# A two-layer decoder trunk on one core: the value and gate products of the gMLP layer split otherwise, and their order and engines changed

## The chip, the core and the metric

The program runs on one core of a Trainium2 chip. The metric is the device time of one execution in microseconds (us); lower is better. A core has TensorE (PE, matrix products, with its weight loads shown as PEld), VectorE (DVE), ScalarE (ACT) and GpSimd (POOL), each of which works through its own list of instructions in order and waits on semaphores for the others. SyncE (SP) issues the DMA transfers that bring inputs from memory (HBM) into the on-chip SBUF. TensorE writes to PSUM, eight banks of 128 x 512 floats, from which VectorE and ScalarE read.

## The reference

The trunk has 512 tokens of width 1024 and two layers, each a token mixer followed by a squared-ReLU MLP, with RMS norms and residual sums. The first mixer is the one that the change touches:

```python
def gmlp_mixer(h, w_in, ln_g, ln_b, w_s, b_s, w_out):
    z = jax.nn.gelu(h @ w_in)               # 512 x 4096
    u, v = jnp.split(z, 2, axis=-1)         # gates u, values v: 512 x 2048 each
    v = layer_norm(v, ln_g, ln_b)
    v = v.reshape(B, S // CHUNK, CHUNK, GMLP_GROUPS, GMLP_GROUP_DIM)
    w = jnp.where(causal[None], w_s, jnp.zeros((), w_s.dtype))
    s = jnp.einsum('gts,bnsgc->bntgc', w, v) + b_s.T[None, None, :, :, None]
    out = u * s.reshape(B, S, GMLP_WIDTH)
    return out @ w_out
```

The second mixer is forgetting attention; both MLPs have 4096 hidden columns. Everything is float32.

## The kernel before, in words

**Products in three parts.** Each float32 operand is split into a rounded high part and the remainder. ScalarE makes the high part (`wh`, `xh`, `gth`, `vh`), VectorE or GpSimd subtracts it to get the low part (`wl`, `xl`, `gtl`, `vl`), and `mm3` (L297) adds three matmuls, high by high, high by low and low by high. So a weight chunk of 128 x 1024 that arrives by DMA (`raw`) costs ScalarE one instruction (L104) and VectorE one (L105) before TensorE can use it. `Stream` holds the list of all chunks; `take` hands out the next one and splits those up to three ahead, with three `raw` buffers and four pairs of `wh` and `wl`.

**2x2 products.** Where two column blocks and two halves of the contraction are at hand, seven half-size products with sums and differences of the operands (Strassen-Winograd) take the place of eight. The sums of the weights are formed on the chip, and so are those of the tokens (`token_sums`, L456; results `gth`, `gtl`).

**The gMLP layer before** has two sections. In the values section TensorE first makes four plain gate blocks (`pu`, 96 matmuls of 512 columns, two chunks interleaved so that work starts with the first block of `x`), and then, twice, a 2x2 product over two groups of 512 value columns (loop over `n` at L521; tiles `v0a` to `v1d`; 7 x 24 = 168 matmuls of 512 columns each time). Of each group of four weight blocks for such a product the four sums are made by `sum_parts` (L449) on GpSimd. `keep` and `join` (L523, L527) move the results to `v`, apply GELU and take statistics. In the gates section come two plain gate blocks (`("u", 2)` in `GMLP_ORDER`, 48 matmuls of 512 columns) and five 2x2 gate pairs (`gate_pair`, L579; tiles `da`, `bc`; 7 x 12 = 84 matmuls of 256 columns each; their weight sums, L133 to L136, on GpSimd). Between these, `mix(cb)` (L642) treats one block of 128 value columns: four ScalarE instructions normalise it (L655, by `lnr` and `lnm`), one makes its high part (L658), GpSimd the low part (L659), TensorE multiplies by the causal weights (`sp`, eight matmuls, L671 and L672), VectorE adds the terms (L661, L674, L675), GpSimd multiplies by the gate `u` (L677), and the result is split into `zg` and `zl` (L684, L685). `out_chunk` (`po`) multiplies four such blocks by the output weights, 24 matmuls of 512 columns for each of 16 chunks, and adds to `x`. The squared sums of the norm go through GpSimd and four small matmuls (`nps`), the spread root through four more (`npb`).

**What sets the order.** `GMLP_ORDER` is the order in which the Python code issues pairs ("uu"), single mixes ("s"), mixing weights ("w") and output chunks ("o"); the numbers in a "uu" entry are the mixes after its four quarters. The scheduler that builds the program then places each engine's instructions, and moves them ahead where it reckons them ready; `tc.issue_after(x)` keeps it from placing an instruction ahead of `x`. Engines run their lists strictly in this order on the chip. The later parts, the MLPs and the attention layer, have an order of their own.

Of the kernel before, what the change touches and what calls it, by code (L numbers as in the profile page):

```python
# [8 lines left out]
F32 = mybir.dt.float32  # L9
# [53 lines left out]
class Stream:  # L63
# [22 lines left out]
    def _load(self):  # L86
# [8 lines left out]
        if i not in self.halved:  # L95
            self.issued[i] = self.nc.sync.dma_start(t[:, :n], src)

    def piece(self, i, e):
        t, n = self.raw[i]
        sl = self._pieces(i, n)[e]  # L100
        self.nc.sync.dma_start(t[:, sl], self.chunks[i][0][:, sl])
# [5 lines left out]
    def _split(self):  # L107
# [17 lines left out]
        if isinstance(src, tuple) and src in self.after:  # L125
            self.after.pop(src)()
# [48 lines left out]
def trunk(ctx: ExitStack, tc: tile.TileContext, A, out, stages=4):  # L175
# [226 lines left out]
    nm = Norm(0)  # L402
    for b in range(KB):
        nm.block(b, squared=False)
        if b == 0:
            ws.prefetch(2)
        if b == 3:
            fourth = nm.high.ins

    with ExitStack() as st:  # L410
# [13 lines left out]
        def u_place(b, dt, name):  # L424

            n, e = divmod(b, 2)
            if n == 0:
                return small.tile([P, S], dt, tag="sqs", name=f"{name}{b}", bufs=2)
            if n in (1, 5):
                return gp.tile([P, S], dt, tag=f"u1_{e}", name=f"{name}{b}")  # L430
            return gq.tile([P, S], dt, tag=f"u{(n - 2) % 4}_{e}", name=f"{name}{b}")
# [6 lines left out]
        with ExitStack() as st2:  # L438
# [4 lines left out]
            def load_part(n, q, c):  # L443
                g, at = {1: (1, 2), 2: (0, 0), 4: (0, 2), 3: (1, 0)}[q]
                t = vp.tile([P, CHUNK_COLS], F32, tag=f"s{q}_{c}", name=f"gs{n}_{q}_{c}")
                nc.sync.dma_start(t, A["gw_v"][2 * n + g, at + c])
                parts[n, q, c] = ws.made[n, q, c] = t

            def sum_parts(n, c):  # L449
                s1, s2, s4, s3 = (parts[n, q, c] for q in (1, 2, 4, 3))  # L450
                pool.tensor_tensor(s1, s3, s1, op=ALU.add)
# [20 lines left out]


            pu = [psA(f"pu{b}") for b in range(4)]
            two = [[t.rearrange("p (k m) -> p k m", m=P) for t in ws.take()] for _ in range(2)]
            for k in range(KB):
                for b, (wh, wl) in enumerate(two):
                    mm3(pu[b], wh[:, k], wl[:, k], nm.h[k], nm.l[k], k == 0, k == KB - 1)
            with tc.issue_after(fourth):
                for b in range(KB):  # L480
                    nm.square(b)
            with tc.issue_after(ws.issued[3].ins):
                for c in range(2):
                    for q in (3, 1, 2, 4):
                        load_part(0, q, c)
            dense_a(pu[2], ws.take(), nm)
            nm.finish()
            with tc.issue_after(nm.squared.ins):
                for k in range(4):
                    token_sums(k)  # L490
            with tc.issue_after(nm.root.ins):
                for c in range(2):
                    sum_parts(0, c)
            dense_a(pu[3], ws.take(), nm)
            nm.spread()
            for b in range(4):
                us[b] = u_place(b, F32, "u")
                gated(pu[b], us[b])
# [16 lines left out]
            def columns(i, g):  # L515
                return v[g][:, :, i]

            def blocks(t):
                return t.rearrange("p (b n) -> p b n", n=P)

            for n in range(2):  # L521

                def keep(i, j, src):  # L523
                    for e in range(2):
                        act.activation(columns(2 * j + e, 2 * n + i), blocks(src[e]), AF.Copy)

                def join(i, j, src):  # L527
                    for e in range(2):
                        t, g = 2 * j + e, 2 * n + i
                        vs = columns(t, g)  # L530
                        dve.tensor_tensor(vs, blocks(src[e]), vs, op=ALU.add)
                        act.activation(vs, vs, AF.Gelu_apprx_tanh, scale=nm.rstd[:, t : t + 1])
                        dve.bn_stats(bn[:, t, g], vs)

                pairs = {}

                def bank(w, *kinds):
                    pairs[w] = [kind(f"v{n}{w}{e}") for e, kind in enumerate(kinds)]

                if n == 0:  # L540
                    bank("a", psB, psB), bank("b", psB, psD), bank("d", psA, psA), bank("c", psA, psA)
                else:
                    bank("c", psB, psB), bank("b", psB, psD), bank("d", psA, psA), bank("a", psA, psA)
                a, b, c_, d = (pairs[w] for w in "abcd")
                if n == 0:
                    for q in (1, 2, 4, 3):
# [690 lines left out]
```

## Time and profile before

| | before |
|---|---|
| median of 3 runs | 1299.96 us (1299.83 to 1300.64) |
| the profiled execution | 1299.96 us, span 1298.2 us |
| TensorE busy | 1258.0 us, 97% of the span |
| VectorE busy | 921.9 us, 71% |
| ScalarE busy | 688.3 us, 53% |
| GpSimd busy | 552.8 us, 43% |
| mean granted clock of TensorE | 0.993 |

The profile is of one execution. Times in its views count from the start of the span. A view by stretches gives each engine's busy time in it; a timeline lists instructions with start and duration, and in brackets the idle time before one and what ended it; a view of waits adds up that idle time by what ended it; a view of groups gives count, total and mean duration by line and operation. Matmuls overlap in the pipeline, so what one costs is the distance between starts, not its duration.

### The profile page before, as it was taken

The page shows a single profiled execution, that of the slowest core. Times are in us where ns is not written, and L with a number is a line of the kernel's source. Part 1 is how long each engine was busy: PE and PEld are TensorE (multiplying, and loading weights), DVE is VectorE, ACT ScalarE, POOL GpSimd, SP SyncE. Part 2 cuts the span into 40 slices and gives each one's busy share as a digit, 9 for nine tenths or more (in the row PEclk, how much of TensorE's full clock was granted, in tenths as well). Part 3 has the DMA queues.
Part 4 walks back from the last instruction along what each step waited for, and adds up shares of the span by engine and source line. Part 5 has one row for each costly group of instructions (what it writes and reads, how often), then busy time and mean ns, then how long its engine had stood idle before and what let it go on. Part 6 is the DMA issues. An engine that isn't in the chain of part 4 may idle for free.

```text
span 1298.2 us, 18918 instructions
## 1 busy us (share of the span) xinstructions
PE 1258.0 (97%) x7247; PEld 1112.1 (86%) x7247; DVE 921.9 (71%) x1190; ACT 688.3 (53%) x1121; POOL 552.8 (43%) x422
## 2 busy tenths in 40 slices
PE   8699789999999999999999999999999999999998
PEld 7477778878889998999899999899788989999987
DVE  7988687898777676675635666766897867676763
ACT  6565864437444444343457777778474434444430
POOL 4762535635532323230357666667364422222200
PEclk9899999999999999999999999999999999999999
DMA  8352133232333232323223223223313332332321
GB/s 325 109 176 69 37 101 109 61 121 81 101 111 113 82 116 80 131 79 117 67 82 124 90 86 102 82 81 99 98 56 123 100 112 98 98 112 84 114 82 65
DMA packets 43595, 132.21 MB, mean 102 GB/s; under 512 B 5416, under 2 KB 7520, under 8 KB 43504
## 3 DMA queue, kind: packets, MB, share of 16 engines
q1 hardware_dynamic: 43216, 130.98, 31.2%
q8 instruction: 57, 0.93, 0.3%
q14 instruction: 34, 0.28, 0.1%
q10 hardware_dynamic: 288, 0.02, 0.0%
HBM read 128.82 MB, written 2.16 MB: 101 GB/s over the span
## 4 chain that ended last, share of the span: by engine, by line
PE 83%; DVE 8%; ACT 4%; issue 2%; POOL 2%; DMA 1%; SPq 0%; DVEq 0%; POOLq 0%; ACTq 0%
PE po L290 36%; PE da L290 12%; PE bc L290 9%; PE pq L290 9%; PE pg L290 3%; PE ph L290 3%; DVE wl L105 2%; PE ot L290 2%; PE lg L290 2%; ACT v L655 1%; PE v1a L290 1%; PE tp L295 1%; PE pv L290 1%; PE v0a L290 1%; PE v1c L290 1%
## 5 line engine op out<-in xcount | busy, mean ns | idle before, releaser
L104 ACT ACTIVATE wh<-raw 128x1024 fp32r<-128x1024 f32 (+3 forms) x236 | 223.8, 950 | 207.8 <-PE po L290 96.3
L105 DVE TENSOR_TENSOR wl<-raw,wh 128x1024 fp32r<-128x1024 f32 (+1 forms) x184 | 274.4, 1506 | 19.9 <-ACT wh L104 19.5
L290 PE MATMUL po<-zl,wh 128*128 128x512 f32 x640 | 251.5, 393 | 2.0 <-DVE zl L747 1.2
L290 PE MATMUL po<-zh,wl 128*128 128x512 f32 x512 | 201.9, 394 | 0.0
L290 PE MATMUL po<-zh,wh 128*128 128x512 f32 x512 | 199.7, 391 | 0.0
L803 DVE TENSOR_TENSOR x<-x,po 128x512 f32<-128x512 f32 x128 | 87.2, 682 | 105.5 <-PE po L290 105.4
L105 POOL TENSOR_TENSOR wl<-raw,wh 128x768 fp32r<-128x768 f32 (+3 forms) x52 | 103.2, 1985 | 125.1 <-ACT wh L104 122.6
L146 POOL TENSOR_TENSOR ssum<-raw 128x512 f32<-128x512 f32 x26 | 36.4, 1400 | 270.0 <-DMA raw<-in_m_dram 260.4
L290 PEld LDWEIGHTS po<-zl,wh 128*128 128x128 f32 x640 | 120.5, 188 | 25.1 <-DVE zl L747 1.5
L104 ACT ACTIVATE sh<-ssum 128x1024 fp32r<-128x1024 f32 x52 | 55.2, 1061 | 163.2 <-POOL ssum L147 94.4
L290 PEld LDWEIGHTS po<-zh,wl 128*128 128x128 f32 x512 | 96.3, 188 | 19.1
L290 PEld LDWEIGHTS po<-zh,wh 128*128 128x128 f32 x512 | 96.4, 188 | 18.2
L290 PE MATMUL pq<-wh,xh 128*128 128x384 f32 (+2 forms) x256 | 88.2, 344 | 0.0
L290 PE MATMUL pq<-wh,xl 128*128 128x384 f32 (+2 forms) x256 | 83.1, 325 | 0.0
L290 PE MATMUL pq<-wl,xh 128*128 128x384 f32 (+2 forms) x256 | 82.9, 324 | 0.0
L105 DVE TENSOR_TENSOR sl<-ssum,sh 128x1024 fp32r<-128x1024 f32 x52 | 65.9, 1268 | 17.7 <-ACT sh L104 17.6
L148 POOL TENSOR_TENSOR ssum<-raw,ssum 128x512 f32<-128x512 f32 x26 | 37.2, 1430 | 66.7 <-DVE sl L105 66.3
L290 PE MATMUL da<-th,sl 128*128 128x256 f32 x208 | 58.9, 283 | 0.0
L290 PE MATMUL da<-tl,sh 128*128 128x256 f32 x208 | 58.7, 282 | 0.0
L290 PE MATMUL da<-th,sh 128*128 128x256 f32 x208 | 58.7, 282 | 0.0
L783 DVE TENSOR_TENSOR zc<-da,sl 128x512 f32<-128x512 f32 x26 | 18.0, 692 | 55.2 <-PE da L290 55.2
L149 POOL TENSOR_TENSOR ssum<-raw,raw 128x512 f32<-128x512 f32 x26 | 56.2, 2162 | 0.0
(336 smaller groups left out, 3658.5 us busy)
## 6 DMA issues: line engine op xcount, KB each, us to landing
raw<-in_m_dram SPq DMA_DIRECT2D x128, 512.0 KB, 3.7
gs<-in_gw_v_dram SPq DMA_DIRECT2D x16, 512.0 KB, 5.7
raw<-in_gw_o_dram SPq DMA_DIRECT2D x16, 512.0 KB, 3.6
raw<-in_fw_qkv_dram SPq DMA_DIRECT2D x20, 384.0 KB, 3.2
raw<-in_gw_u_dram SPq DMA_DIRECT2D x14, 512.0 KB, 3.6
raw<-in_gw_v_dram SPq DMA_DIRECT2D x12, 512.0 KB, 3.6
raw<-in_fw_g_dram SPq DMA_DIRECT2D x8, 512.0 KB, 3.5
cb<-cd SPq DMA_DIRECT2D x16, 256.0 KB, 3.3
```

The costliest lines, as they stand in the source:

```text
L104: self.nc.scalar.activation(hi, t, AF.Copy)
L105: eng.tensor_tensor(lo, t, hi.bitcast(F32), op=ALU.subtract)
L146: tt(s12[:, 0], a21, a22, op=ALU.add)
L148: tt(s43[:, 0], a12, s12[:, 1], op=ALU.subtract)
L149: tt(s43[:, 1], a11, a21, op=ALU.subtract)
L290: ins = pe.matmul(dst, a, b, start=start, stop=stop, skip_group_check=more)
L295: placed(pe.transpose(dst, src, ident[: src.shape[0], : src.shape[0]]), 256)
L655: act.activation(vb[:, i], vb[:, i], AF.Identity, scale=lnr[:, i : i + 1], bias=lnm[:, i : i + 1])
L783: dve.tensor_tensor(z[:, 1].rearrange("p (j t) -> p j t", j=2), a.unsqueeze(1).to_broadcast([P, 2, HS]), late.rearrange("p (j t) -> p j t" ...
L803: dve.tensor_tensor(x[b], x[b], pt, op=ALU.add)
```

## The change

The values section starts with plain products for the first two groups of 512 columns (192 matmuls of 512 columns, tiles `pv`), and only the other two groups are a 2x2 product (168). Their weight sums, now eight instructions in place of sixteen, are on VectorE. The four plain gate blocks at the start and the two in the gates section are gone: all 16 gate blocks are eight 2x2 pairs (8 x 84 matmuls of 256 columns), all after the values. The two first chunks of the stream are still loaded in halves. The normalising instructions of block `cb` may stand no earlier than behind the high part of block `cb - 1`. Line numbers move by 5 to some 35 (the splits L104 and L105 become L99 and L100, `mm` L290 becomes L275).

```diff
-GMLP_ORDER = [("w", 0), ("u", 2), ("uu", 3, None, 0, 1, 2), ("uu", 4, 3, None, None, None)]
-GMLP_ORDER += [("o", 0, 0), ("s", 4), ("o", 0, 1), ("s", 5), ("o", 0, 2), ("o", 0, 3)]
...
+GMLP_ORDER = [("w", 0), ("uu", 0, None, None, None, None), ("uu", 1, None, None, 0, None), ("uu", 2, None, 1, 2, None)]
+GMLP_ORDER += [("uu", 3, 3, None, None, None), ("o", 0, 0), ("s", 4), ("o", 0, 1), ("s", 5), ("o", 0, 2), ("o", 0, 3)]
+GMLP_ORDER += [("uu", 4, 6, 7, None, None), ("w", 1), ("o", 1, 0), ("o", 1, 1)]
...
-    ws.load(2)
     load_x(0)
-    ws.piece(0, 0)
-    ws.piece(1, 0)
...
+    ws.load(1)
+    for b in range(1, KB):
         load_x(b)
...
+            def load_parts(c):
+                for q, (g, at) in ((3, (3, 0)), (1, (3, 2)), (2, (2, 0)), (4, (2, 2))):
+                    parts[q, c] = ws.made[q, c] = vp.tile([P, CHUNK_COLS], F32, tag=f"s{q}_{c}", name=f"gs{q}_{c}")
+                    nc.sync.dma_start(parts[q, c], A["gw_v"][g, at + c])
+
+            def sum_parts(c):
+                s1, s2, s4, s3 = (parts[q, c] for q in (1, 2, 4, 3))
+                dve.tensor_tensor(s1, s3, s1, op=ALU.add)
+                dve.tensor_tensor(s3, s2, s3, op=ALU.subtract)
+                dve.tensor_tensor(s2, s1, s2, op=ALU.subtract)
+                dve.tensor_tensor(s4, s4, s2, op=ALU.subtract)
...
+            def normal(i, g, src):
+                vs = columns(i, g)
+                act.activation(vs, src, AF.Gelu_apprx_tanh, scale=nm.rstd[:, i : i + 1])
+                dve.bn_stats(bn[:, i, g], vs)
+
+            for g in range(2):
+                pv = [(psB if g == 1 and i < 3 else psA)(f"pv{g}_{i}") for i in range(NT)]
+                for c in range(4):
+                    wh, wl = (t.rearrange("p (k n) -> p k n", k=2) for t in ws.take())
+                    for i in range(NT):
+                        for kk in range(2):
+                            k = 2 * c + kk
+                            mm3(pv[i], nm.h[k][:, tok[i]], nm.l[k][:, tok[i]], wh[:, kk], wl[:, kk], k == 0, k == KB - 1)
...
+                    if g == 0 and c > 1:
+                        with tc.issue_after(ws.issued[2 * c + 2].ins):
+                            load_parts(c - 2)
+                    if g == 1 and c in (1, 2):
+                        sum_parts(c - 1)
...
+            with tc.issue_after(now["vh"]) if cb else ExitStack():
+                for i in range(NT):
+                    act.activation(vb[:, i], vb[:, i], AF.Identity, scale=lnr[:, i : i + 1], bias=lnm[:, i : i + 1])
...
+            now["vh"] = act.activation(vh, vb, AF.Copy).ins
...
+            with tc.issue_after(lnm_made.ins):
+                dve.scalar_tensor_tensor(b2, now["rs"][:, g * P : (g + 1) * P], lngb[:, 1, cb : cb + 1], now["b"], op0=ALU.mult, op1=ALU.add)
```

**Three places in the built order.** First GpSimd before, in the values section, behind the root of the norm (`rstd`); `gs` are the weight blocks of a 2x2 product:

```order
L344 TENSOR_TENSOR rstd_344<-ms_342,mhalf 128x4
L451 TENSOR_TENSOR gs_1_0_293<-gs_3_0_291,gs_1_0_293 128x1024
L451 TENSOR_TENSOR gs_1_1_301<-gs_3_1_299,gs_1_1_301 128x1024
L452 TENSOR_TENSOR gs_3_0_291<-gs_2_0_295,gs_3_0_291 128x1024
L452 TENSOR_TENSOR gs_3_1_299<-gs_2_1_303,gs_3_1_299 128x1024
L453 TENSOR_TENSOR gs_2_0_295<-gs_1_0_293,gs_2_0_295 128x1024
```

Now VectorE has them, between the splits (`wl`) and the token sums (`t`, `gt`, `gtl`) of the same section:

```order
L444 TENSOR_TENSOR t_377<-gx_375 128x256
L446 SCALAR_TENSOR_TENSOR t_377<-x_91,gains,t_377 128x256
L445 SCALAR_TENSOR_TENSOR gt_376<-x_91,gains,gx_375 128x256
L431 TENSOR_TENSOR gs_0_332<-gs_0_330,gs_0_332 128x1024
L100 TENSOR_TENSOR wl_341<-raw_166,wh_340 128x1024
L447 SCALAR_TENSOR_TENSOR gt_376<-x_91,gains,t_377 128x256
L451 TENSOR_TENSOR gtl_201<-t_377,gth_197 128x512
L432 TENSOR_TENSOR gs_0_330<-gs_0_334,gs_0_330 128x1024
```

The sums have left GpSimd's list and stand one by one among VectorE's other work. Second, ScalarE before, at the first mix; `v` are the value blocks, `vh` the high part of one, `u` a gate:

```order
L436 ACTIVATE u_1079<-u_1079 128x512
L655 ACTIVATE v_175<-v_175,lnm,lnr 128x128 x16
L655 ACTIVATE v_176<-v_176,lnm,lnr 128x128
L658 ACTIVATE vh_1198<-v_175 128x512
L104 ACTIVATE wh_1116<-raw_937 128x1024
L655 ACTIVATE v_176<-v_176,lnm,lnr 128x128
L436 ACTIVATE u_1113<-u_1113 128x512
```

and now:

```order
L417 ACTIVATE u_980<-u_980 128x512
L623 ACTIVATE v_193<-v_193,lnm,lnr 128x128 x4
L99 ACTIVATE wh_951<-raw_825 128x1024
L626 ACTIVATE vh_1118<-v_193 128x512
L623 ACTIVATE v_193<-v_193,lnm,lnr 128x128 x2
L417 ACTIVATE u_981<-u_981 128x512
L623 ACTIVATE v_193<-v_193,lnm,lnr 128x128 x2
L555 ACTIVATE gse_1010<-da_1008 128x256
```

Four normalisations stand ahead of the first high part, in place of seventeen. Third, VectorE now, at the first mix (`sp` to `zt`) in the second gate pair, with the splits of the weights that follow:

```order
L643 SCALAR_TENSOR_TENSOR zt_1124<-sp_0_1125,lngb,b_1122 128x256
L643 SCALAR_TENSOR_TENSOR zt_1124<-sp_1_1132,lngb,b_1122 128x256
L644 SCALAR_TENSOR_TENSOR zt_1124<-sp_0_1125,lngb,zt_1124 128x256
L644 SCALAR_TENSOR_TENSOR zt_1124<-sp_1_1132,lngb,zt_1124 128x256
L630 SCALAR_TENSOR_TENSOR b_1307<-rs_1109,lngb,bs_1297 128x128
L100 TENSOR_TENSOR wl_1001<-raw_803,wh_1000 128x1024
L100 TENSOR_TENSOR wl_1005<-raw_926,wh_1004 128x1024
```

and TensorE there (`da` is half of the pair's result):

```order
L641 MATMUL sp_1_1132<-wsb_873,vl_1119 128x128
L640 MATMUL sp_1_1132<-wsb_873,vh_1118 128x256
L641 MATMUL sp_1_1132<-wsb_873,vl_1119 128x128
L275 MATMUL da_1008<-gth_197,wh_1000 128x256
L275 MATMUL da_1008<-gtl_201,wh_1000 128x256
L275 MATMUL da_1008<-gth_197,wl_1001 128x256
```

The split `wl_1001`, which the third product behind the mix needs, stands on VectorE behind the five instructions of the mix.

More of the change, by code (lines that the diff above doesn't have):

```diff
@@ L94, in _load @@
         self.raw[i] = (t, n)
[L95 to L101, printed above, removed]
+        for sl in self._pieces(i, n):
+            self.issued[i] = self.nc.sync.dma_start(t[:, sl], src[:, sl])
     def _parts(self, hi, lo, t, eng):
@@ L424, in u_place @@
         def u_place(b, dt, name):
[L426 to L431, printed above, removed]
+            return gq.tile([P, S], dt, tag=f"u{b % 8}", name=f"{name}{b}")
         def gated(pu, u):
@@ L471, in token_sums @@
                     dve.tensor_tensor(l, t, h.bitcast(F32), op=ALU.subtract)
[L474 to L498, printed above, removed]
+            def columns(i, g):
+                return v[g][:, :, i]
+            def blocks(t):
+                return t.rearrange("p (b n) -> p b n", n=P)
+            def normal(i, g, src):
+                vs = columns(i, g)
+                act.activation(vs, src, AF.Gelu_apprx_tanh, scale=nm.rstd[:, i : i + 1])
+                dve.bn_stats(bn[:, i, g], vs)
@@ new lines, in trunk @@
+            for g in range(2):
+                pv = [(psB if g == 1 and i < 3 else psA)(f"pv{g}_{i}") for i in range(NT)]
[5 more added lines that the diff above has]
+                            mm3(pv[i], nm.h[k][:, tok[i]], nm.l[k][:, tok[i]], wh[:, kk], wl[:, kk], k == 0, k == KB - 1)
+                    if g == 0 and c == 2:
+                        with tc.issue_after(fourth):
+                            for b in range(KB):
+                                nm.square(b)
+                        nm.finish()
+                    if g == 0 and c == 3:
+                        nm.spread()
+                        with tc.issue_after(nm.squared.ins):
+                            for k in range(4):
+                                token_sums(k)
+                    if g == 0 and c > 1:
[4 more added lines that the diff above has]
+                for i in range(NT):
+                    normal(i, g, blocks(pv[i]))
@@ L513, in sums @@
                 return lambda k: [t[k][:, q - 1] for t in (th, tl)]
[L515 to L546, printed above, removed]
-                        for c in range(2):
-                            ws.after[0, q, c] = lambda q=q, c=c: load_part(1, q, c)
-                product(a, half(0, 0))
-                keep(0, 0, a)
-                product(b, half(1, 0))
-                join(0, 0, b)
-                product(d, sums(4))
-                keep(1, 0, d)
-                product(c_, sums(1))
-                keep(1, 1, c_)
-                product(a, sums(2), True)
-                keep(0, 1, a)
-                product(c_, half(1, 1), True)
-                if n == 0:
-                    for c in range(2):
-                        sum_parts(1, c)
-                join(0, 1, c_)
-                product(a, sums(3), True)
-                join(1, 0, a)
-                join(1, 1, a)
@@ new lines, in trunk, with keep, join @@
+            a, b = ([psA(f"v{w}{e}") for e in range(2)] for w in "ab")
+            c_, d = [psB(f"vc{e}") for e in range(2)], [psB("vd0"), psD("vd1")]
+            def keep(i, j, src):
+                for e in range(2):
+                    act.activation(columns(2 * j + e, 2 + i), blocks(src[e]), AF.Copy)
+            def join(i, j, src):
+                for e in range(2):
+                    vs = columns(2 * j + e, 2 + i)
+                    dve.tensor_tensor(vs, blocks(src[e]), vs, op=ALU.add)
+                    normal(2 * j + e, 2 + i, vs)
@@ L568, in trunk @@
+            product(a, half(0, 0))
+            keep(0, 0, a)
+            product(b, half(1, 0))
+            join(0, 0, b)
+            product(d, sums(4))
+            keep(1, 0, d)
+            product(c_, sums(1))
+            keep(1, 1, c_)
+            product(a, sums(2), True)
+            keep(0, 1, a)
+            product(c_, half(1, 1), True)
+            join(0, 1, c_)
+            product(a, sums(3), True)
+            join(1, 0, a)
+            join(1, 1, a)
         gq = st.enter_context(tc.tile_pool(name="gq", bufs=1))
@@ L689, in trunk @@
         for kind, n, *at in GMLP_ORDER:
[L690 to L696 removed]
+            if kind == "w":
                 mixing_weights(n)
```

64 lines of the change are left out of this document (17 added, 47 removed).

## The prediction

> **What bounds the kernel now.** I read the span, then busy time by stretches, then TensorE's waits, then the timelines around the two longest, and last the prices.
>
> ```profile
> span 1298.2 us, 18918 instructions
> ```
> The profiled execution took 1299.96 us, exactly the median of the three runs; 1.8 us lie outside its span. From the first MLP on, all engines have the same instructions in the same order before and after, so only the gMLP layer, the first 311.9 us, can change of itself. The stretches follow; the columns are length, then busy time of TensorE, its weight loads, VectorE, ScalarE and GpSimd, then the granted clock.
>
> ```profile
> 0.00:311.90 311.90, 280.94 (x1450) 236.79 (x1451) 253.43 (x308) 176.46 (x284) 158.11 (x94) 0.97 0.37 121
> 30.95:125.75 94.80, 81.61 (x346) 64.62 (x344) 84.84 (x72) 53.99 (x70) 55.67 (x20) 0.95 0.39 123
> 125.75:311.90 186.15, 171.71 (x987) 150.01 (x986) 146.16 (x207) 102.31 (x182) 89.85 (x61) 0.98 0.28 85
> 137.00:171.00 34.00, 22.97 (x149) 20.66 (x148) 21.45 (x30) 34.00 (x80) 13.47 (x11) 0.91 0.20 61
> 250.00:275.00 25.00, 21.59 (x135) 18.72 (x134) 24.76 (x34) 13.31 (x22) 12.79 (x9) 1.00 0.42 127
> ```
> TensorE is the bound, yet idle for 31 us of the layer (311.9 less 280.94): 13.2 us in the values (second row), 14.4 us in the gates (third), 11.0 of these between 137 and 171, where ScalarE is busy all the time. TensorE's waits, longest first (total, times, longest):
>
> ```profile
> PE v0a L290 <- DVE wl L105: 10.6, 1, 10.6
> PE po L290 <- ACT wh L104: 4.0, 1, 4.0
> PE sp L671 <- DVE zt L675: 3.0, 3, 1.5
> PE sp L671 <- DVE u L607: 2.3, 1, 2.3
> ```
> The 10.6 us end with VectorE's split at 42.33. VectorE's and GpSimd's timelines (start, duration) show why:
>
> ```profile
> 23.50 0.86 DVE L464 TENSOR_TENSOR t<-gx 128x256 f32<-128x256 f32 x1 [1.94 <-ACT gx L460]
> ...
> 31.78 2.88 DVE L471 TENSOR_TENSOR gtl<-gt,gth 128x512 fp32r<-128x512 f32 x1
> ...
> 42.33 3.36 DVE L105 TENSOR_TENSOR wl<-raw,wh 128x1024 fp32r<-128x1024 f32 x1
> ...
> 124.29 1.22 DVE L105 TENSOR_TENSOR wl<-raw,wh 128x1024 fp32r<-128x1024 f32 x1 [0.43 <-ACT wh L104]
> ```
> ```profile
> 31.62 5.26 POOL L451 TENSOR_TENSOR gs<-gs,gs 128x1024 f32<-128x1024 f32 x2
> ```
> A split takes 1.22 us with GpSimd quiet and 3.36 us beside GpSimd's weight sums of 2.63 us each. The second idle stretch begins after this:
>
> ```profile
> 125.43 2.48 DVE L531 TENSOR_TENSOR v<-v1a,v 128x512 f32<-128x512 f32 x4
> ```
> ```profile
> 136.00 6.66 ACT L655 ACTIVATE v<-v,lnm,lnr 128x128 f32<-128x128 f32 x17 [3.13 <-DVE lnm L577]
> ```
> From the last value join to the first normalisation are 10.6 us; then ScalarE makes 17 normalisations (0.39 us each) before it forms the first block's high part.
>
> **The change part by part.** Prices of TensorE are starts over count in the chain of waits: 24 value products, 24 plain gate products, 24 half-width ones, 24 of the output. Then the first and last row of four of a mix's eight products.
>
> ```profile
> 109.24 5.60 PE v1a L290 x24
> ...
> 125.91 5.48 PE pu L290 x24
> ...
> 235.31 2.85 PE da L290 x24
> ...
> 306.59 5.49 PE po L290 x24
> ```
> ```profile
> 144.75 0.33 PE L671 MATMUL sp<-wsb,vh 128*128 128x256 f32 x1
> ...
> 145.26 0.22 PE L672 MATMUL sp<-wsb,vl 128*128 128x128 f32 x1
> ```
> That is 0.233, 0.228, 0.119 and 0.229 us, and 2 x 0.51 = 1.0 us a mix. The marks of the layer are its first product, the sum of squares (0.8 us, and the spread of the root as much), the first gate product and the first of the MLP:
>
> ```profile
> 5.17 0.51 PE L290 MATMUL pu<-xh,wh 128*128 128x512 f32 x1 [0.39 <-ACT wh L104]
> ...
> 27.73 0.95 PE L290 MATMUL nps<-ones,sqs 128*128 128x2 f32 x8
> ...
> 125.75 0.39 PE L290 MATMUL pu<-xh,wh 128*128 128x512 f32 x1
> ...
> 311.93 0.40 PE L290 MATMUL ph<-xh,wl 128*128 128x512 f32 x1
> ```
>
> Products. Three plain gate pairs leave (144 x 0.228 = 32.9 us) and three split ones come (252 x 0.119 = 29.9); a plain value pair has 24 products more (5.6 us). TensorE gains 2.6 us of work.
>
> Values before: 5.2 + 96 x 0.228 + 336 x 0.233 + 1.6 = 107.1; they ended at 125.75, so 18.7 us were waiting and low clock. After: the first product still needs only the first x block and the first half chunk, in the same place of the queue; a step of k then takes 12 products (2.8 us) for 512 KB, where six products (1.4 us) took 384 KB. I allow 0.5 us of waits and get 5.2 + 360 x 0.233 + 1.6 + 0.5 = 91.3.
>
> VectorE's sums are eight instructions; the nearest row is the undisturbed split of the same size, 8 x 1.22 = 9.8 us; the upper bound is 8 x 3.36 = 26.9, the lower nothing, while GpSimd is quiet. Three of them stand before the split of the eighth chunk, which TensorE needs after 170 products, at about 46.5. VectorE reaches its first token sum at about 23.5 as now (the first row), and has some 11 us of sums, splits and token sums up to the end of that split: 12 us of cover. At the upper bound of the three sums (10.1 for 3.7) 5 us are left; behind it the splits for the 2x2 pair take VectorE 1.22 us per 2.8 us of TensorE. So nothing on the path, and up to 10 us if that cover is gone.
>
> Gates before: 125.75 + 48 x 0.228 + 420 x 0.119 + 384 x 0.229 + 0.9 + 16 x 1.0 = 291.6, with 0.9 for the four row-sum products; they ended at 311.9, so 20.3 us waited. After, the work is 672 x 0.119 + 87.8 + 0.9 + 16.3 = 184.8, which would end at 276.1. What waits are left decides. VectorE's rows in the gate stretch (total, mean ns of one):
>
> ```profile
> L105 DVE TENSOR_TENSOR wl<-raw,wh 128x1024 fp32r<-128x1024 f32 x33 | 48.9, 1488 | 5.1 <-ACT wh L104 5.0
> L388 DVE TENSOR_TENSOR x<-x,po 128x512 f32<-128x512 f32 x31 | 20.4, 678 | 12.6 <-PE po L290 12.6
> L675 DVE SCALAR_TENSOR_TENSOR zt<-sp,lngb,zt 128x256 f32<-128x256 f32 x32 | 14.0, 473 | 0.0
> L674 DVE SCALAR_TENSOR_TENSOR zt<-sp,lngb,b 128x256 f32<-128x256 f32 x32 | 13.9, 476 | 0.7
> L685 DVE TENSOR_TENSOR zl<-zt,zg 128x512 fp32r<-128x512 f32 x16 | 12.9, 803 | 8.0 <-ACT zg L684 7.9
> L435 DVE TENSOR_TENSOR u<-u,rbc 128x512 f32<-128x512 f32 x10 | 12.1, 1213 | 0.1
> ...
> L661 DVE SCALAR_TENSOR_TENSOR b<-rs,lngb,bs 128x128 f32<-128x128 f32 x16 | 5.4, 340 | 5.5 <-PE rs L648 5.5
> L105 DVE TENSOR_TENSOR wl<-raw,wh 128x512 fp32r<-128x512 f32 x5 | 5.0, 1002 | 0.3 <-ACT wh L104 0.3
> ...
> L435 DVE TENSOR_TENSOR u<-pu,rbc 128x512 f32<-128x512 f32 x2 | 1.4, 692 | 1.0 <-PE pu L290 0.9
> ```
> A split pair costs VectorE 3 x 1.488 + 1.002 + 2 x 0.678 + 2 x 1.213 = 9.2 us, a mix 0.34 + 2 x 0.476 + 2 x 0.473 + 0.803 = 3.0, an output chunk 1.488 + 2 x 0.678 = 2.8. The first four pairs with four mixes have 49 us of VectorE against 45 of TensorE (336 x 0.119 + 4.1 + 0.9): at least 4 us of waiting. Step by step it is more. The chain from the last join to the first high part is 10.6 + 4 x 0.39 + 0.6 = 12.8 us; two full and one half split of the gates now stand in it (4.0), so it ends 16.8 us after the values, while TensorE comes to the first mix after 129 half-width products and the row sums, 15.8; the third weights of the second pair then wait on ScalarE behind those normalisations: 2.5 us in all. Next, TensorE needs the split of the second pair's last weights, and VectorE has four instructions of the mix (1.9), one of 0.34 and that split (1.49) in a row: 3.3 us. The third pair repeats a third of this (1.1), the first and fourth lose 0.5 and 1.0. Sum 8.4 us. The upper bound is the present hand-over, 11.0 us idle over two pairs, so 22 for four.
>
> The last four pairs, twelve mixes and the output have 140 us of TensorE beside 118 of VectorE, with output chunks between the pairs; two pairs back to back lost 3.4 us (250 to 275). I take 2, from 0 to 7. Low clock and gaps too small for the list: 2.5, since 34 us at 0.91 cost about 3. The layer then ends at 276.1 + 8.4 + 2 + 2.5 = 289.0, earlier than 311.9 by 22.9; 1299.96 - 22.9 gives **1277 us**.
>
> Normalising a block ahead costs nothing: the same 64 instructions in another order; its new wait holds ScalarE's other work only behind a high part that is due first.
>
> The low clock has a page: the Trainium skill, TensorE: Matmul & The Clock Gate, HAM oscillation, has the clock drop only after idle gaps over about 3.4 us. By it none of the waits that I expect would cost clock, and the sum would be 1274.5. In the stretch at 0.91 the longest wait was 4.0 us, so this trace does not contradict it.
>
> **The rivals.** *A, nearly no waits in the gates* (0 to 6 us): for it, the stretch after 235 packed two pairs with little loss; against it, VectorE's 49 against 45. 1264 to 1270.
> *B, the hand-over keeps its stall*: the last values still come just before the gates, and if each VectorE instruction there meets a GpSimd one, the first four pairs lose up to 22 us. 1284 to 1291.
> *C, the sums on VectorE delay the values*: up to 10 us, 1287; it needs weights that land 12 us late.
> *D, slower*: VectorE becomes the bound of all eight pairs. Between ends far apart: splits, gatings and low parts with both inputs in SBUF are 80; if each waited for a whole GpSimd operation,
>
> ```profile
> 128.59 1.29 POOL L133 TENSOR_TENSOR raw<-raw 128x512 f32<-128x512 f32 x1 [7.48 <-DVE wl L105]
> ```
> then 1.29 us over the undisturbed 1.22 (or 0.69), VectorE would need 146 + 23 for the new pairs + 80 = 249 us for the gates: 1328. It decides once VectorE passes 221 us, 0.65 us more on each. Against it: the gating with one input in PSUM (692) and with two in SBUF (1213) differ by 0.52, which these means hold already, and GpSimd has only 64 such operations.
> The Trainium skill, SBUF — State Buffer, Who interferes with whom, says that a VectorE instruction with two SBUF inputs and a GpSimd one that reads SBUF exclude each other for a whole instruction. The two gating rows agree. By it the pair of them would need 64 x 1.29 + 48 x 1.22 + 32 x 0.69 = 163 us at most of the 185, so D could not happen.
> *E, no effect* (1300): the stalls have other causes than these; the split of 3.36 us beside the sums speaks against it.
>
> **How the numbers follow.** Forecast (1271 to 1284) 0.60, A 0.15, B 0.14, C 0.04, D 0.05, E 0.02. A measurement of this kernel tells 0.2% (2.6 us) from no change. Faster are the forecast, A, B and C: 0.93; same is E, 0.02; slower D, 0.05. The range takes in A and most of B: 1266 to 1290.
>
> **What would show it.** Right: no wait over 1 us in the values; the first gate product near 91; the MLP's first near 289; splits of 1.2 us beside sums of the same length on VectorE; after the first mix, a wait of some 3 us for a split. Wrong: a wait of the values for the sums or their loads; normalisations still in a row; VectorE above 95% over all gate pairs.

## The result, and the profile after

The changed kernel takes 1281.74 us (median of 4 runs, 1281.25 to 1282.32) against 1299.89 us (1299.49 to 1300.64) for the kernel before on the same chip: a ratio of 0.986 with a 95% interval of 0.9843 to 0.9877. That is 18.2 us less, where 22.9 were forecast. The profiled execution took 1282.32 us, with 1280.6 in its span.

The first view of after is by stretches: the whole layer, its values, its gates and outputs, and the two halves of the latter (length, then busy time of TensorE, its weight loads, VectorE, ScalarE and GpSimd, then the granted clock).

```profile
0.00:294.20 294.20, 281.93 (x1582) 247.21 (x1583) 235.56 (x314) 174.01 (x288) 130.60 (x90) 0.98 0.36 118
5.26:91.61 86.35, 85.41 (x377) 70.07 (x377) 70.38 (x84) 54.52 (x75) 23.83 (x14) 1.00 0.49 171
91.61:294.20 202.59, 192.74 (x1191) 173.65 (x1190) 164.25 (x228) 116.45 (x208) 106.08 (x71) 0.97 0.30 94
106.00:153.00 47.00, 38.01 (x252) 35.75 (x251) 37.68 (x45) 34.00 (x68) 30.75 (x19) 0.85 0.28 81
153.00:294.20 141.20, 140.34 (x824) 123.60 (x823) 112.29 (x160) 73.77 (x124) 68.56 (x46) 1.00 0.32 100
```

The values now have 0.9 us without TensorE work (13.2 before), and the second half of the gates 0.9. Nearly all that is left stands in 47 us, between 106 and 153: TensorE is idle for 9.0 us there and has a mean clock of 0.85. The marks are the spread of the root, the first gate product, the longest wait and the first product of the MLP (the form that stood at 311.93):

```profile
36.87 1.16 PE L275 MATMUL npb<-ident,rstd 128*128 128x128 f32 x8 [0.94 <-POOL rstd L329]
...
91.61 0.28 PE L275 MATMUL da<-gth,wh 128*128 128x256 f32 x1
...
114.29 0.58 PE L275 MATMUL da<-gth,wl 128*128 128x256 f32 x1 [2.85 <-DVE wl L100]
...
294.26 0.39 PE L275 MATMUL ph<-xh,wl 128*128 128x512 f32 x1
```

311.93 - 294.26 = 17.7 us is the whole gain of the span (1298.2 - 1280.6 = 17.6): nothing changed behind the layer. TensorE's waits of the layer (total, times, longest), without those of the first 6 us:

```profile
PE da L275 <- DVE wl L100: 4.0, 3, 2.8
PE da L275 <- ACT wh L99: 2.3, 2, 1.9
PE sp L640 <- DVE zt L644: 2.1, 1, 2.1
...
PE npb L275 <- POOL rstd L329: 0.9, 1, 0.9
```

VectorE's timeline (start, duration), where the sums (`gs`) and the splits (`wl`) now stand together, shows both at 1.22 to 1.23 us:

```profile
28.16 1.23 DVE L431 TENSOR_TENSOR gs<-gs,gs 128x1024 f32<-128x1024 f32 x1 [1.03 <-DMA gs<-in_gw_v_dram]
29.30 1.22 DVE L100 TENSOR_TENSOR wl<-raw,wh 128x1024 fp32r<-128x1024 f32 x1
...
33.51 0.16 DVE L327 TENSOR_SCALAR ms<-nps 128x4 f32<-128x4 f32 x1
```

In the gates it is not so. The split behind the first mix stands beside GpSimd's multiplication by the gate (`zt`) and a low part (`vl`) behind it:

```profile
111.99 2.25 DVE L100 TENSOR_TENSOR wl<-raw,wh 128x1024 fp32r<-128x1024 f32 x1
```
```profile
111.89 1.26 POOL L646 TENSOR_TENSOR zt<-zt,u 128x512 f32<-128x512 f32 x1 [2.41 <-ACT wh L99]
```
It takes 2.25 us, 1.0 more than in the values, and it is the split that ends TensorE's longest wait (2.85 us, at 114.29).

The clock of the stretch from 106 to 153 is read in windows of 3.41 us, because the half clock in this trace begins and ends on such a grid:

```profile
106.08:109.49 3.41, 2.57 (x17) 1.95 (x17) 1.49 (x2) 3.41 (x8) 3.22 (x2) 1.00 0.09 19
109.49:112.90 3.41, 1.46 (x11) 1.11 (x10) 2.75 (x6) 3.41 (x7) 1.01 (x1) 1.00 0.41 149
112.90:116.31 3.41, 2.02 (x9) 2.02 (x10) 3.41 (x2) 3.20 (x8) 2.48 (x2) 0.51 0.28 74
116.31:119.73 3.42, 3.42 (x18) 3.42 (x17) 1.63 (x4) 1.53 (x4) 2.51 (x2) 0.50 0.20 79
...
136.79:140.20 3.41, 1.26 (x11) 1.11 (x11) 3.41 (x6) 1.71 (x3) 2.75 (x3) 1.00 0.00 0
140.20:143.62 3.42, 3.42 (x18) 3.42 (x18) 1.58 (x3) 3.03 (x8) 3.42 (x2) 0.51 0.27 22
143.62:147.03 3.41, 1.55 (x13) 1.35 (x12) 3.07 (x7) 1.89 (x3) 2.64 (x3) 0.99 0.33 135
147.03:150.44 3.41, 3.41 (x15) 3.12 (x15) 3.41 (x3) 2.79 (x6) 1.70 (x2) 0.51 0.42 65
```

Behind each window in which TensorE was busy for 1.3 to 1.6 of 3.4 us stands one at half clock; the window at 106.08, busy for 2.57, has none behind it. TensorE works for 2.02 + 3.42 + 3.42 + 3.41 = 12.3 us at half clock; at full clock the same work takes half of that, so the half clock costs 6.1.

### The profile page after: what moved, and what is told of

Same layout as the page of the kernel before. It is cut to its first block, busy times and chain, and to the rows that moved or that the text cites. A ratio compares the mean times of both kernels' runs of the same rounds, so it can differ in the third digit from the quotient of the medians.

```text
span 1280.6 us, 19160 instructions
## 1 busy us (share of the span) xinstructions
PE 1259.1 (98%) x7379; PEld 1122.6 (88%) x7379; DVE 903.5 (71%) x1196; ACT 686.0 (54%) x1125; POOL 524.0 (41%) x418
## 4 chain that ended last, share of the span: by engine, by line
PE 82%; DVE 7%; POOL 3%; issue 3%; ACT 2%; DMA 1%; SPq 0%; DVEq 0%; POOLq 0%; ACTq 0%
PE po L275 35%; PE da L275 13%; PE bc L275 10%; PE pq L275 9%; PE pg L275 3%; PE ph L275 3%; DVE wl L100 2%; PE pv L275 2%; PE ot L275 2%; PE lg L275 1%; PE va L275 1%; PE tp L280 1%; PE vc L275 1%; ACT wh L99 1%; POOL zt L646 1%
## 5 line engine op out<-in xcount | busy, mean ns | idle before, releaser
L99 ACT ACTIVATE wh<-raw 128x1024 fp32r<-128x1024 f32 (+3 forms) x244 | 229.8, 947 | 199.0 <-PE po L275 82.1
L100 DVE TENSOR_TENSOR wl<-raw,wh 128x1024 fp32r<-128x1024 f32 (+1 forms) x192 | 274.1, 1442 | 24.1 <-ACT wh L99 23.5
L275 PE MATMUL po<-zl,wh 128*128 128x512 f32 x640 | 251.8, 394 | 1.4 <-DVE zl L710 1.4
L275 PE MATMUL po<-zh,wl 128*128 128x512 f32 x512 | 201.9, 394 | 0.0
L275 PE MATMUL po<-zh,wh 128*128 128x512 f32 x512 | 199.6, 391 | 0.0
L100 POOL TENSOR_TENSOR wl<-raw,wh 128x768 fp32r<-128x768 f32 (+3 forms) x52 | 103.2, 1986 | 125.0 <-ACT wh L99 122.5
L99 ACT ACTIVATE sh<-ssum 128x1024 fp32r<-128x1024 f32 x52 | 55.2, 1061 | 163.1 <-issue 93.2
L275 PEld LDWEIGHTS po<-zl,wh 128*128 128x128 f32 x640 | 120.8, 189 | 24.0 <-DVE zl L710 1.6
L275 PEld LDWEIGHTS po<-zh,wl 128*128 128x128 f32 x512 | 96.4, 188 | 19.0
L275 PEld LDWEIGHTS po<-zh,wh 128*128 128x128 f32 x512 | 96.4, 188 | 18.2
L275 PE MATMUL pq<-wh,xh 128*128 128x384 f32 (+2 forms) x256 | 88.2, 344 | 0.0
L275 PE MATMUL pq<-wh,xl 128*128 128x384 f32 (+2 forms) x256 | 83.1, 325 | 0.0
L275 PE MATMUL pq<-wl,xh 128*128 128x384 f32 (+2 forms) x256 | 82.9, 324 | 0.0
L100 DVE TENSOR_TENSOR sl<-ssum,sh 128x1024 fp32r<-128x1024 f32 x52 | 66.0, 1268 | 18.1 <-ACT sh L99 18.0
L275 PE MATMUL da<-th,sl 128*128 128x256 f32 x208 | 59.0, 283 | 0.0
L275 PE MATMUL da<-th,sh 128*128 128x256 f32 x208 | 58.8, 282 | 0.0
L275 PE MATMUL da<-tl,sh 128*128 128x256 f32 x208 | 58.7, 282 | 0.0
```

What stands on the lines that cost most here:

```text
L99: self.nc.scalar.activation(hi, t, AF.Copy)
L100: eng.tensor_tensor(lo, t, hi.bitcast(F32), op=ALU.subtract)
L275: ins = pe.matmul(dst, a, b, start=start, stop=stop, skip_group_check=more)
```

## The experiments

Each time is a median of 4 runs, with the ratio to the kernel before on the same chip in brackets (1299.3 to 1299.8 us in these runs).

**The sums back on GpSimd** (e1).

```diff
-                dve.tensor_tensor(s1, s3, s1, op=ALU.add)
+                pool.tensor_tensor(s1, s3, s1, op=ALU.add)
```
(and so the three below it)

> The changed kernel with its eight weight sums back on GpSimd, all else as it is (1281.7 us). Theory of the prediction (the sums on GpSimd stretch VectorE's splits from 1.22 to 3.36 us, but two plain groups of values leave about 12 us of cover): splits of over 2 us beside sums of 2.6 us reappear between 28 and 60 us, TensorE waits at most 2 us for them, 1281 to 1284 us. Rival one (the engine of the sums is what removed the wait of 10.6 us): a wait of 5 to 10 us in the values, 1287 to 1292 us. Rival two (VectorE, busy 22.1 of 22.2 us from 38 to 60, has too much there): the sums off VectorE make it faster, 1278 to 1281 us.

Measured: 1287.99 us, 1285.19 to 1288.86 (0.9906, 0.9890 to 0.9923), 6.3 more than the change. Splits are stretched again, but TensorE waits for none of them: it waits for the root of the norm. VectorE, TensorE and GpSimd of this run:

```profile
29.45 3.42 DVE L100 TENSOR_TENSOR wl<-raw,wh 128x1024 fp32r<-128x1024 f32 x1
...
38.24 0.15 DVE L327 TENSOR_SCALAR ms<-nps 128x4 f32<-128x4 f32 x1
```
```profile
42.01 2.07 PE L275 MATMUL npb<-ident,rstd 128*128 128x128 f32 x8 [5.71 <-POOL rstd L329]
```
```profile
38.48 3.48 POOL L329 TENSOR_TENSOR rstd<-ms,mhalf 128x4 f32<-128x4 f32 x1 [3.35 <-DVE ms L327]
```
The mean square `ms` stands behind stretched work on VectorE and comes at 38.24 in place of 33.51; the root takes until 42; the wait is 5.7 us, 4.8 longer, and a half clock follows it. Rival one's time and its wait of 5 to 10 us came out, but in a place that none of the three had named: the cover of 12 us was there for the splits, not for the root.

**The sums on VectorE in the kernel before** (e2), the same edit of `sum_parts` the other way round.

> The kernel before with its sixteen weight sums moved from GpSimd to VectorE, all else as it is (1299.9 us). Theory of the prediction (the wait of 10.6 us is VectorE's split stretched by GpSimd's sums, in a place without cover): the splits fall to 1.2 us, but VectorE gets eight sums of 1.22 us ahead of that split, 9.8 us for about as much that it lost to stretching; the wait stays at 6 to 11 us, 1295 to 1302 us. Rival (the engine of the sums alone makes the wait): the wait falls under 3 us, 1288 to 1293 us.

Measured: 1288.47 us, 1288.18 to 1289.08 (0.9916, 0.9901 to 0.9931). The rival was right: 11 us less from the engine of the sums alone. The wait of 10.6 us is gone; what stands there is

```profile
PE npb L290 <- POOL rstd L344: 2.0, 1, 2.0
```
My sum had counted the stretch of one split. In the kernel before, six VectorE instructions in a row alternate with six sums of GpSimd: the two quoted in the prediction (2.88 and 3.36) and these.

```profile
34.70 2.46 DVE L465 SCALAR_TENSOR_TENSOR gt<-x,gains,gx 128x256 f32<-128x256 f32 x1
37.08 2.56 DVE L467 SCALAR_TENSOR_TENSOR gt<-x,gains,t 128x256 f32<-128x256 f32 x1
39.57 2.84 DVE L471 TENSOR_TENSOR gtl<-t,gth 128x512 fp32r<-128x512 f32 x1
...
45.61 2.59 DVE L464 TENSOR_TENSOR t<-gx 128x256 f32<-128x256 f32 x1
```
They take 16.7 us; undisturbed the six forms take 0.69, 0.48, 0.48, 0.69, 1.22 and 0.43, in sum 4.0. In e2 seven sums stand ahead of that split on VectorE, 1.21 us each but for the first two, from 21.83 on, and the split starts at 37.44 and takes 1.21 us:

```profile
37.44 1.21 DVE L105 TENSOR_TENSOR wl<-raw,wh 128x1024 fp32r<-128x1024 f32 x1
```
So 12.7 us of stretching were exchanged for sums that VectorE began 10 us earlier.

**No hold on the normalising** (e3).

```diff
-            with tc.issue_after(now["vh"]) if cb else ExitStack():
-                for i in range(NT):
+            for i in range(NT):
```

> The changed kernel without the rule that the normalising of a block stands behind the high part of the one ahead; its built order has 16 normalisations ahead of the first high part instead of four. Theory (ScalarE is on the path at the first mix): the first high part comes 12 x 0.39 = 4.7 us later and the later ones earlier, 1283 to 1288 us. Rival (VectorE's split behind the mix decides, ScalarE has time): no change, 1280 to 1283 us.

Measured: 1287.40 us, 1287.2 to 1288.96 (0.9910, 0.9895 to 0.9924), 5.7 more. ScalarE's timeline and TensorE's:

```profile
103.47 5.89 ACT L622 ACTIVATE v<-v,lnm,lnr 128x128 f32<-128x128 f32 x15 [0.55 <-DVE lnm L544]
```
```profile
110.35 0.58 PE L275 MATMUL bc<-gth,wh 128*128 128x256 f32 x1 [4.58 <-ACT wh L99]
...
281.49 0.98 PE L275 MATMUL po<-zg,wh 128*128 128x512 f32 x3 [1.91 <-ACT zg L652]
```
The theory holds in its place: 15 normalisations in a row, and TensorE waits 4.58 us behind them. But the last mixes also moved in the built order, and there TensorE waits 1.9 us and has one half-clock window (1.7 us): 3.6 of the 5.7 us are not of the first mix.

**The hold alone, in the kernel before** (e4), the same edit the other way round.

> The kernel before with that rule alone: normalising a block ahead, four in place of 17 ahead of the first high part. Theory (the 17 normalisations in a row make the 11.0 us of idle TensorE between 137 and 171): the waits for ScalarE there (4.0 and 1.9 us, 0.9 for the low part) go, about 5 to 8 us less, 1292 to 1295 us. Rival (VectorE's instructions of the mix and its splits take over at once): 1296 to 1300 us.

Measured: 1294.96 us, 1292.42 to 1297.70 over 10 runs (0.9965, 0.9956 to 0.9975): 4.5 less, at the edge of the theory's range. Those waits for ScalarE went; one of 2.6 us for VectorE's `zt` and one of 1.9 for its `u` stand in their place.

**Both in the kernel before** (e9): e2 and e4 together.

> The kernel before with two parts of the change, the sixteen sums on VectorE and the normalising a block ahead; the values stay two 2x2 products, the gates six plain blocks and five 2x2 pairs. By adding what the two did alone (11.0 and 4.5 us): 1284 us, and then the exchange of products is worth 2 to 3 us. Rival one (they meet in the same waits): 1286 to 1289 us. Rival two (the exchange of products costs more than it gives): 1281 us or less.

Measured: 1285.24 us, 1281.46 to 1286.47 (0.9884, 0.9865 to 0.9903). The two nearly add. By the medians the exchange of products (values half plain, all gate pairs as 2x2) is then worth 3.5 us; one run of e9 took 1281.46, as little as the change, so this part is not clear of the spread of 5 us between e9's runs.

**ScalarE relieved** (e5) and **VectorE relieved** (e6) in the first four mixes.

```diff
-                for i in range(NT):
+                for i in range(NT if cb > 3 else 0):
```
```diff
-                dve.scalar_tensor_tensor(zc, s4[:, :, 1], gcol, zc, op0=ALU.mult, op1=ALU.add)
+                if cb > 3:
+                    dve.scalar_tensor_tensor(zc, s4[:, :, 1], gcol, zc, op0=ALU.mult, op1=ALU.add)
```

> The changed kernel (1281.7 us) without the 16 normalising instructions of the first four blocks: this part of the computation is left out, and ScalarE has 16 x 0.39 = 6.2 us less between 104 and 119 us. Theory (VectorE's list decides: split behind the mix, two terms of a mix behind other work): the waits for VectorE of 2.8 and 2.1 us stay, those for ScalarE (0.5 and 1.9) go, 1277 to 1281 us. Rival (ScalarE's list decides the stretch from 106 to 152, in which 18 us are lost): the loss falls under 9 us, 1273 us or less.

> The changed kernel without the second of the two terms that VectorE adds in each half of the first four mixes (the low part of the mixing weights is left out there): eight instructions of 0.47 us, 3.8 us of VectorE less between 110 and 150 us, nothing less on ScalarE or TensorE. Theory (VectorE's list decides there): 4 to 6 us less, the lower clock behind the waits among them, 1275 to 1278 us. Rival (ScalarE's list decides): 1280 to 1283 us.

Measured: e5 1277.19 us, 1276.62 to 1279.02 (0.9828, 0.9814 to 0.9843); e6 1280.78 us, 1279.47 to 1281.49 (0.9852, 0.9838 to 0.9867). The stretch from 106 to 153 in e5, then in e6:

```profile
106.00:153.00 47.00, 41.29 (x299) 38.77 (x298) 39.31 (x52) 28.87 (x53) 31.01 (x19) 0.96 0.33 106
```
```profile
106.00:153.00 47.00, 40.26 (x270) 36.85 (x270) 39.02 (x44) 34.98 (x70) 31.95 (x19) 0.93 0.31 96
...
273.43:276.84 3.41, 1.39 (x6) 1.06 (x7) 0.69 (x1) 0.63 (x1) 1.26 (x1) 1.00 0.47 154
276.84:280.25 3.41, 3.41 (x10) 2.64 (x9) 3.08 (x4) 2.94 (x5) 0.00 (x0) 0.51 0.00 0
```
Both gain in the stretch: idle time falls from 9.0 to 5.7 and 6.7 us, and half-clock windows from four to one and two. e6 gives 3.7 us of that back at 273, where the last mix, again in another place of the built order, makes TensorE wait 2.0 us and lose a window. So e5 fits the theory's range only from its lower edge, and e6 by its total fits the rival and by its stretch the theory.

Of the two waits for VectorE that the theory said would stay in e5, one did (2.04 us for `zt`, for 2.15) and one did not: behind the first mix TensorE waits 1.08 us for ScalarE's `gsl` in place of 2.85 for a split, and that split, at 110.96, takes 1.21 us in place of 2.25. VectorE's splits between 91.6 and 153 us, in the change and then in e5:

```profile
L100 DVE TENSOR_TENSOR wl<-raw,wh 128x1024 fp32r<-128x1024 f32 x13 | 21.5, 1680 | 2.6 <-ACT wh L99 2.6
```
```profile
L100 DVE TENSOR_TENSOR wl<-raw,wh 128x1024 fp32r<-128x1024 f32 x14 | 18.0, 1297 | 3.8 <-ACT wh L99 3.8
```
So e5 does not relieve ScalarE alone: in its order, in which the first mix also stands some products earlier, the splits are stretched less. Neither engine alone is shown to carry the loss, and these two runs don't settle their shares.

**TensorE kept busy in its waits** (e8).

```diff
+        def fill(name, n, after):
+            t = psB(name)
+            with tc.issue_after(after):
+                for _ in range(n):
+                    pe.matmul(t, nm.h[0][:, :P], nm.h[0], start=True, stop=True)
...
+                if (cb, c) in ((0, 1), (3, 0)):
+                    fill(f"fill{cb}", 8 if cb == 0 else 7, last)
...
+            if n == 3:
+                fill("fillp", 6, order["last"])
```

> The changed kernel with 21 products that nobody reads put into three of TensorE's waits (8 behind the first mix, 7 and 6 in the fourth pair; 1.8, 1.6 and 1.4 us at 0.228 us each, in waits of 2.8, 2.1 and 1.9 us). Theory (the half clock for 6.7, 3.3 and 3.3 us behind these waits is a cost of its own): the granted clock stays near 1, 2 to 5 us less, 1276.5 to 1280 us. Rival (a faster TensorE would only wait longer for VectorE): the clock stays near 1 and the time within 1281 to 1283 us. A third way: the products come where TensorE doesn't wait, up to 4.8 us more.

Measured: 1277.06 us, 1276.9 to 1277.4 (0.9825, 0.9809 to 0.9842): 4.7 less, by 21 products more. The whole stretch and, on this run's own grid, its least busy window with the one behind it:

```profile
106.00:153.00 47.00, 41.98 (x297) 38.23 (x298) 38.45 (x49) 34.32 (x70) 31.82 (x19) 1.00 0.29 94
111.76:115.17 3.41, 1.69 (x14) 1.63 (x14) 3.41 (x2) 3.41 (x9) 2.88 (x2) 1.00 0.22 42
115.17:118.59 3.42, 3.42 (x31) 3.42 (x30) 3.39 (x5) 1.62 (x5) 2.10 (x2) 1.00 0.29 111
```
The idle 5.0 us and the 4.8 us of filling make 9.8, about as much as the idle 9.0 of the change; the clock stays at 1.00 in this trace, and the mean clock is 1.00 in each of the four runs. The 4.7 us are therefore the clock's, most of the 6.1 worked out above: a faster TensorE did not just wait longer.

**Plain gate pairs beside the mixes**: two (e7) and one (e7b).

```diff
-... ("uu", 2, None, 1, 2, None)]
-GMLP_ORDER += [("uu", 3, 3, None, None, None), ("o", 0, 0), ...
+... ("u", 2, 1, 2)]
+GMLP_ORDER += [("u", 3, 3, None), ("o", 0, 0), ...
```
("u" makes two plain blocks, with a mix behind each; e7b keeps the entry of pair 3)

> The changed kernel with the third and fourth gate pair as plain products again, the first mixes behind their blocks: TensorE has 2 x (48 x 0.228 - 84 x 0.119) = 1.9 us more, VectorE 2 x (9.2 - 4.4) = 9.6 us less over the first four pairs, 39 us in place of 49 against 47 of TensorE. Theory (VectorE's work per pair makes the loss of 18 us): at least 8 of the 18 us go, 1271 to 1276 us. Rival (a delay of hand-over, whatever the pairs beside it): the 1.9 us are added, 1282 to 1286 us.

> The changed kernel with the third gate pair alone as plain products, mixes 1 and 2 behind its two blocks, mix 3 in the fourth pair as it is: TensorE has 1.0 us more, VectorE 4.8 less (44 us in place of 49 against 46). Theory (VectorE's work over the first four pairs sets the loss, in proportion): about half of the gain of two plain pairs (10.3 us), 1275 to 1278 us. Rival (the loss goes as soon as VectorE has less than TensorE): 1270 to 1273 us.

Measured: e7 1271.45 us, 1270.8 to 1273.2 (0.9784, 0.9769 to 0.9798), the fastest of all; e7b 1273.16 us, 1272.75 to 1274.77 (0.9800, 0.9785 to 0.9814). Two windows of the change, then of e7:

```profile
100.00:120.00 20.00, 15.82 (x105) 14.86 (x104) 15.52 (x21) 14.04 (x30) 14.91 (x10) 0.83 0.19 64
120.00:150.00 30.00, 25.19 (x180) 24.12 (x179) 25.47 (x33) 20.19 (x38) 20.28 (x14) 0.89 0.24 61
```
```profile
100.00:120.00 20.00, 16.68 (x106) 14.94 (x106) 16.71 (x21) 15.87 (x32) 11.83 (x8) 0.91 0.32 95
120.00:150.00 30.00, 30.00 (x154) 25.51 (x153) 21.34 (x34) 16.78 (x30) 8.71 (x6) 1.00 0.36 113
```
With plain pairs TensorE has no idle time and the full clock from 120 to 150, for 1.9 us more of work. The loss goes as the theory had it, but not in proportion: one plain pair gives 8.6 of the 10.3 us, nearer to e7b's rival. A plain pair also relieves ScalarE and GpSimd (20.28 to 8.71 us in the second window), so the runs show that the 2x2 pairs beside the first mixes cost the time, not that VectorE alone does.

**The first mixes later**: with two plain pairs (e10: mixes 0 to 3 behind the four plain blocks) and in the change itself (e11: two mixes in the third, two in the fourth pair).

```diff
-("uu", 1, None, None, 0, None), ("u", 2, 1, 2), ("u", 3, 3, None)
+("uu", 1, None, None, None, None), ("u", 2, 0, 1), ("u", 3, 2, 3)
```
```diff
-("uu", 1, None, None, 0, None), ("uu", 2, None, 1, 2, None), ("uu", 3, 3, None, None, None)
+("uu", 1, None, None, None, None), ("uu", 2, None, 0, None, 1), ("uu", 3, None, 2, None, 3)
```

> The version with two plain gate pairs (1271.5 us), with all four first mixes moved behind the four plain blocks, none in the second pair any more. Theory (what is left of the loss, 6.6 us between 100 and 120, stands where a mix meets the splits of a 2x2 pair): 3 to 6 us less, 1266 to 1269 us. Rival (the loss there is the tail of the values: last joins, norm and first splits, mix or no mix): within 1 us of 1271.5.

> The changed kernel (1281.7 us), all pairs 2x2, with the first four mixes later and evenly spread: behind the first and third quarter of the third pair and the second and fourth... of the pairs after it (two mixes in the third pair, two in the fourth, none in the second). VectorE's work over the first four pairs is the same 49 us. Theory (VectorE's work sets the loss, wherever the mixes stand): 1279 to 1283 us. Rival (the early place of the first mix makes it, close behind the last values): 1272 to 1277 us.

Measured: e10 1271.69 us, 1270.26 to 1274.07 (0.9788, 0.9773 to 0.9803), as e7; e11 1280.15 us, 1279.76 to 1280.37 (0.9851, 0.9836 to 0.9866). So e10 fits its rival and not the theory, and e11 the theory and not its rival: in both the place of the mixes matters little. In e10 no mix stands between 100 and 110 any more, and TensorE loses a window all the same:

```profile
107.39:110.80 3.41, 1.62 (x11) 1.42 (x12) 0.81 (x2) 3.41 (x9) 1.76 (x1) 1.00 0.48 143
```
VectorE is busy for 0.8 us there and ScalarE for all 3.4. ScalarE's timeline shows what its high parts of weights (`wh`) stand behind:

```profile
103.91 1.65 ACT L625 ACTIVATE v<-v,lnm,lnr 128x128 f32<-128x128 f32 x4 [0.54 <-DVE lnm L546]
105.47 1.04 ACT L99 ACTIVATE wh<-raw 128x1024 fp32r<-128x1024 f32 x1
```
Four normalisations, which had to wait for `lnm` of the last values, come ahead of a weight that is due. That this order is the rest of the loss was not tried.

## Why the prediction was nearly right, point by point

The direction, the place and most of the size held; the error of 5.3 us in the layer's end (294.3 for 289.0) is one term.

- **Values**: 91.61 for 91.3, no wait over 1 us, sums and splits at 1.22 to 1.24 us from 28 to 59 us. Right. The reason was right in kind (GpSimd's sums stretch VectorE) and too narrow in size: not one split, but six instructions, 12.7 us; and the consumer without cover is the root of the norm, which the prediction didn't name (e1).
- **Rival C** (the sums delay the values) asked for weights 12 us late; the first sum waited 1.03 us for its load. It did not happen.
- **Work of TensorE in the gates**: taken as 184.8 us. The stretch took 294.26 - 91.61 = 202.65, so 17.9 us were lost, where 12.9 were forecast.
- **Waits**: 8.4 + 2 forecast, 202.59 - 192.74 = 9.9 measured. The split behind the first mix waits 2.85 us (3.3 forecast). Its parts were other ones: the split was priced at 1.49 us and took 2.25. The other terms were spread wrongly: 1.3 us up to the third weights of the second pair (2.5), some 0.4 in the third pair (1.1), 2.15 and 1.86 in the fourth (1.0), and 0.9 in the second half (2). That their sum came out is in part luck.
- **Low clock and small gaps**: 2.5 forecast, 17.9 - 9.9 = 8.0 measured, 6.1 of them half clock. This is the step that failed. It was priced from the mean clock of 0.91 in one stretch of the kernel before, as if two short spells would come again; the change has three windows of the grid in which TensorE is less than half busy. e8 takes the spells away and gains 4.7 us. The other 1.9 us were not traced; they are rather more, since the sum has 1.0 us a mix and the eight products of the first mix in e5 take 0.86 without a wait (107.81 to 108.67).
- **The page on the clock**: the Trainium skill, TensorE: Matmul & The Clock Gate, HAM oscillation, gives the rule to leave no idle gaps over some 3.4 us; the prediction read it as saying that the clock drops only after such gaps. The trace disagrees: the longest wait was 2.85 us, and the clock halved at 112.9, 140.2 and 147.0. The Trainium skill, TensorE: Matmul & The Clock Gate, What's actually happening, describes a window of about 3.4 us that runs freely. The grid agrees with that, but the page lets the clock drop after an idle window, and the windows before a drop were 37 to 45% busy here. The trace of the kernel before disagreed with the rule too, which the prediction missed: its longest wait between 137 and 171 was 4.0 us, but that one came at 167, and at 147.89 the clock had already halved, behind a window whose longest wait was 1.45 us:

```profile
144.48:147.89 3.41, 1.57 (x11) 1.31 (x11) 3.41 (x5) 3.41 (x9) 1.32 (x2) 1.00 0.37 108
147.89:151.31 3.42, 3.42 (x16) 3.42 (x17) 2.39 (x4) 3.42 (x9) 2.17 (x2) 0.50 0.19 72
```
```profile
146.94 0.35 PE L671 MATMUL sp<-wsb,vh 128*128 128x256 f32 x1 [1.45 <-DVE zt L675]
```

- **Normalising ahead costs nothing**: right, and it gains: 4.5 us alone in the kernel before.
- **Rivals**: A (nearly no waits) and B (the whole stall stays) lay on either side and neither came; of B the 9.0 us of idle time between 106 and 153 remain, and B's mechanism with them in part: the splits of the gates still meet GpSimd's work (2.25 us behind the first mix). D fell: VectorE was busy for 164 of 202.6 us. By the Trainium skill, SBUF — State Buffer, Who interferes with whom, a VectorE instruction with two SBUF inputs and a GpSimd one that reads SBUF hold each other off for a whole instruction; the six stretched instructions, one to a sum of 2.5 to 3 us, agree. E fell.
- **VectorE's 49 us against 45** as the reason of the hand-over's waits: not shown. e7, e7b and e6's stretch speak for relief of VectorE, e5 for relief of ScalarE (or for splits that meet GpSimd less), e11 against any one place. No run took GpSimd's work out of the gates by itself, so its share is untested. Which engine's work weighs how much stays open; each edit moved the built order too.

## What to carry to other kernels

Price a short wait of TensorE twice: by its length, and by whether it leaves a window of 3.41 us busy for less than some 48%: each time here a half-clock window followed, which costs 1.7 us when it is full of work. When an engine's instructions beside GpSimd's look stretched, add up all of them over the stretch, and ask what else waits behind them. Work that is fewest products is not always the fastest: where mixes, splits and weight sums crowd the other engines, two plain pairs with 1.9 us more of TensorE were 10.3 us faster.

## What the runs showed of the hardware that was not expected

The half clock of TensorE came in spells of one or more windows on a grid of 3.41 us. The grid does not start with the kernel: the first spell begins at 112.94 us in the change, 110.83 in e10 and 109.82 in e11, which is 0.30, 1.60 and 0.59 us past a multiple of 3.413. Laid over the traces of before, after and all twelve experiments (30 to 300 us), 26 windows at full clock were busy for less than 48%, and each was followed by a half-clock window; of 12 between 48 and 60% three were; of 1028 above 60% none was. Out of the half clock: each of 27 half-clock windows that were full (97% and more) was followed by full clock, and each of 12 that were busy for less than 80% by another one at half clock. At 91 to 93% it went either way: full clock came back in e6 behind 113.08, but not in e10 behind 110.80:

```profile
110.80:114.22 3.42, 3.11 (x12) 2.62 (x13) 2.77 (x4) 3.42 (x8) 0.00 (x0) 0.50 0.43 121
```

On GpSimd the power of four columns (`rstd`) took 1.03 us in the kernel before, and beside VectorE's work with two inputs in SBUF 3.08 in the change and 3.48 in e1: the stretching goes both ways.
